# Turning the queries of a delta rule on VectorE and through DRAM instead of on TensorE, and a new order of the mixer's columns

## The chip, the cores and the metric

The kernel runs on one core of a Trainium2 chip. The core has a matrix engine (TensorE, PE in the profile, with its weight loads shown as PEld), VectorE (DVE), ScalarE (ACT), GpSimd (POOL) and SyncE (SP), which only issues transfers. Each engine works through its own list of instructions in order, and they wait for one another by semaphores. The metric is the device time of one execution in microseconds; lower is better.

## The reference

One decoder layer on 512 tokens of 1024 channels, in float32: a feed-forward block, a mixer, a second feed-forward block, a final norm. The mixer projects its input into columns and feeds two branches: a gated linear recurrence with 8 heads (HGRN2), and a gated delta rule with 8 heads of queries and keys and 16 of values. What matters here is how the queries and keys of the delta rule are normalized:

```
qkv = silu(causal_short_conv(concat([gq, gk, gv]), conv_w))
cq, ck, cv = split(qkv)
q_g = l2norm(cq.reshape(B, S, 8, 128)) * 128 ** -0.5      # x * rsqrt(sum(x*x) + eps)
k_g = l2norm(ck.reshape(B, S, 8, 128))
...
o_g = gated_delta_chunked(q_g, k_g, cv, beta, g)          # 64-token chunks in the reference
o_g = rmsnorm(o_g, gdn_out_norm) * silu(gz)
```

So for each token and each of the 8 heads a sum of 128 squares is wanted, of the key and of the query.

## The kernel before

Activations are kept with channels on the 128 partitions and the 512 tokens along the free axis. A float32 product is made of three products of split operands (high and low parts; `mm3`, lines 189 to 192). A weight block is loaded by SP into one of three `raw` tiles, split by ScalarE (line 1819) and VectorE (line 1821), and then used by TensorE.

The mixer computes its input projection column by column: a column is 128 output channels, 24 products of 128x512 into one PSUM bank of the two in lane "mm". The letters of the string `DENSE` name them: Q, F, B are the first branch's, D the decays', k, q, v the delta rule's keys, queries and values, z its output gates, y the first branch's projection; sixteen columns t (merge gates) have no place in the string. The order in `DENSE` is one of preference: `choose` takes the first column in it whose conditions hold (buffers free, a recurrence far enough), and a gate t when none does.

Everything in the mixer is written as threads (generators) that ask for buffers, wait for events and say which engine they need and about how long. At build time a planner (`Desk`) plays these threads through with its own costs, and the order in which it grants an engine becomes the order of instructions on that engine. The columns (`product`) are the thread of least urgency on TensorE and fill what the others leave. Nothing is rearranged on the chip. `V(n)`, `A(n)` and `T_(n)` are the planner's costs for VectorE, ScalarE and TensorE, `S` is one issue on SP, `LAG` holds assumed latencies, `("get", tag, n)` takes buffers of a kind, `D.put` returns them, `D.fire` tells of an event and `("on", ...)` waits for one.

A column of the delta rule goes through `conv` (line 1118): it takes two tiles of the pool `ta`, which has six, copies the product out of PSUM (line 1125), makes the short convolution and the gate. Keys and queries are written to `kq[:, c, i]`, four token blocks c, with the key (i = 0) and the query (i = 1) side by side; values are turned to tokens on partitions with `turn` and `bounce`. `turn` (line 1154) is VectorE's transpose of 32x32 blocks, and `bounce` (line 1158) writes the result to DRAM and reads it back in an order that finishes the transpose (lines 1162 and 1167, both on SP).

The eight pairs u of value heads (one query and key head each) go through these threads:

- `norms(u, i)` (line 1190) makes the sums of squares of the key (i = 0) or query (i = 1): four transposes on TensorE into the PSUM bank of lane "e" (line 1196; there is one such bank), for the key a copy of it to SBUF (line 1199), and four squares on ScalarE, each with its sum over the free axis (line 1203), in place in PSUM. Then the bank is free.
- `g_n` (line 1207) starts both, makes the coefficients from the key's sums, and multiplies keys with keys and queries (`pgq`, line 1242, also in lane "e").
- `g_b` inverts 32x32 triangular blocks on GpSimd (lines 1293 and 1294), `g_inv` joins them to 128x128 inverses on VectorE and TensorE (lines 1312 to 1370).
- `g_rec` (from line 1374) runs the recurrence over the four token blocks, and at its end scales the outputs by factors that hold the query's sums (lines 1472 to 1486).

After the last column, `closing` multiplies the delta rule's outputs with its branch projection; it needs the outputs of all pairs (`so[k]`, lines 1512, 1514, 1604, 1606).

Of the kernel before, what the change touches and what calls it, by code (L numbers as in the profile page):

```python
# [11 lines left out]
AF = mybir.ActivationFunctionType  # L12
# [6 lines left out]
NT = T // P  # L19
D = 1024  # L20
# [11 lines left out]
LEVELS = (1, 2, 4, 8, 16)  # L32

DENSE = (
# [3 lines left out]
)  # L38
MERGE = (None, None, "a", "a", "b", "b", None, None)
WB = 6  # L40
# [11 lines left out]
FRESH = 5  # L52
LAG = dict(raw=3.5, gb=6.5, nb=6, m=7, out=6.5, back=6, turn=6.5)
EASE = 2.5
LANES = {"a": 2, "b": 2, "d": 1, "e": 1}


# [84 lines left out]
def body(tc, xT, cst, sqc, hmask, dta, w1o, w1a, w2a, wt, wn, wab, wbh, wbg, wo, w1b, w2b, yT, dbg=None):  # L142
# [51 lines left out]
    def dense(src, nk, xs, m=P, n=T, lane=None):  # L194
# [3 lines left out]
        else:  # L198
            pt = psc.tile([P, T], F32, tag="p" + lane, name="pmm", bufs=LANES[lane])
        k = 0  # L200
# [154 lines left out]
    def fast(w, p, xo, fp, at, posts, gate):  # L355
# [17 lines left out]
        def prod(o, c, new=None):  # L373
            def run(hi, lo):
                if new:
                    v["pt"] = psc.tile([P, T], F32, tag="p" + new, name="px", bufs=LANES[new]) if new != "m" else \
                        psd.tile([P, T], F32, tag="mm", name="px")
# [71 lines left out]
    def ffn(w1, w2, c0, after, slow, lead=None, last=None):  # L449

        with tc.tile_pool(name="ff", bufs=1) as fp, \
# [6 lines left out]
            mm = lambda: psd.tile([P, T], F32, tag="mm", name="pmm")  # L458
            lane = lambda x: lambda: psc.tile([P, T], F32, tag="p" + x, name="pmm", bufs=LANES[x])

# [107 lines left out]
    def opening(pl):  # L568
# [17 lines left out]

        pw = psc.tile([P, T], F32, tag="pe", name="pwarm", bufs=LANES["e"])
        for i in range(11):
            pe.matmul(pw[:, :P], ones, ones, start=True, stop=True)
        pts = [psd.tile([P, T], F32, tag="mm", name="pmm") for _ in range(2)]  # L590
        pts += [psc.tile([P, T], F32, tag="pa", name="pmm", bufs=LANES["a"]) for _ in range(2)]
        parts = []
# [29 lines left out]
    def last(go, pl, units, on, hooks):  # L622
# [7 lines left out]
        for q in range(2):  # L630
# [21 lines left out]
            def scale(c=c, r=r):  # L652
                pb = psc.tile([P, T], F32, tag="pe", name="pbc", bufs=LANES["e"])
                for i in range(2):
                    pe.matmul(pb[:, i * P:(i + 1) * P], r[:, i:i + 1].to_broadcast([P, P]), ident,
                              start=True, stop=True)
                act.copy(rbc[:, c], pb[:, :256])
                for kt in range(KD):
                    g = cs[:, C_FN + kt:C_FN + kt + 1]
                    if kt % 2 == 0:  # L660
                        o = pl.tile([P, T], F32, name="rw", bufs=RW).rearrange("p (a t) -> p a t", a=2)
                    if kt in scaled:
                        pool.tensor_tensor(o[:, 1], h[:, kt, c], rbc[:, c], op=ALU.mult)
                    else:
                        dve.scalar_tensor_tensor(o[:, kt % 2], h[:, kt, c], g, pb[:, :256], op0=ALU.mult, op1=ALU.mult)
                    if kt % 2 == 1:
                        sp.dma_start(yT[:, kt - 1:kt + 1, c], o)
# [21 lines left out]
def mixer(tc, mp, e):  # L689
    nc = tc.nc  # L690
    pe, act, dve, pool, sp = nc.tensor, nc.scalar, nc.vector, nc.gpsimd, nc.sync
# [6 lines left out]
    def ps(name, lane="d"):  # L698
        return psc.tile([P, T], F32, tag="p" + lane, name=name, bufs=LANES[lane])

    def v3(ap, a):
        return ap.rearrange("p (a b) -> p a b", a=a)
# [9 lines left out]
    def alloc(tag, bufs):  # L712
        def f(name, shape=(P, T), dt=F32):
            return mp.tile(list(shape), dt, tag=tag, name=name, bufs=bufs)
        return f
    op = [alloc(f"op{i}", 1) for i in range(8)]
    ta = alloc("ta", TA)
# [3 lines left out]
    for size, names in ((1024, "n2:2 gz:2 fs:1 ut:1"), (512, "kn:3 gm:1 qm:2 gb:2 ln:1 at:4 vb:4 t64:2 on:2"),  # L721
                        (256, "ft:1 tp:1 thg:2 x:1 we:1 s:3 w:1"), (128, "fm:1"), (64, "sm:4")):
        for it in names.split():
            n, b = it.split(":")
# [35 lines left out]
    D = Desk(wx0=1, wx1=1, wx2=1, wx3=1, mm=2, a=2, b=2, d=1, e=1, ta=TA, tm=6, thg=1, raw=RB, w=WB, n2=2, gz=2, fs=1, ut=1, t=3, kn=3, gm=1,  # L760
             qm=2, gb=2, ln=1, mi=3, mt=3, at=4, vb=4, t64=2, on=2, ft=1, x=1, we=1, w_=1, s=3)
    V = lambda n: ("use", "DVE", 0.21 + 0.001 * n)
    A = lambda n: ("use", "ACT", 0.2 + 0.0009 * n)
# [169 lines left out]
    def h_head(i):  # L933
# [151 lines left out]
        dve.tensor_scalar(rho, ss, 4.0 / P, 4.0 * EPS * 4.0 * P, op0=ALU.mult, op1=ALU.add)  # L1085
        yield "lag", EASE
        yield "use", "POOL", 1.2
        pool.tensor_tensor(rho, rho, mhalf[:, :NT], op=ALU.pow)
        yield "lag", EASE
        for c in range(NT):  # L1090
# [29 lines left out]
    def conv(k, i, pt, out, n):  # L1120
# [22 lines left out]
        if n:  # L1143
            dve.scalar_tensor_tensor(out, a, 1.0, b, op0=ALU.add, op1=ALU.mult)
            D.put("ta", 2)
        else:
            dve.scalar_tensor_tensor(y, a, 1.0, b, op0=ALU.add, op1=ALU.mult)
            yield V(512)
            turn(th, y)
            D.put("ta")  # L1150
            yield from bounce(f"vn{i}", th, out, "ta")
        D.fire(k)

    def turn(out, x):

        dve.transpose(out.rearrange("p (f c j) -> p f c j", f=4, c=NT), x.rearrange("p (c i f) -> p f c i", c=NT, f=4))

    def bounce(name, x, out, tag=None):

        yield S  # L1160
        scr = dr.tile([P, T], F32, name=name)
        sp.dma_start(scr, x)
        yield "lag", LAG["turn"]
        if tag:
            D.put(tag)
        yield S
        sp.dma_start(out.rearrange("p (r a) -> p r a", r=4), scr.rearrange("(r i) (f a) -> (i f) r a", r=4, f=4))
        yield "lag", LAG["turn"]
# [20 lines left out]

    def norms(u, i, kq, kn, sm):  # L1190
        yield "on", ("kq"[i], u)
        yield "get", "e", 1
        yield T_(Patient(.5))
        pt = ps("ptk", "e")
        for c in range(NT):
            pe.transpose(pt[:, c * P:(c + 1) * P], kq[:, c, i], ident)
        if i == 0:
            yield A(512)
            act.copy(kn, v3(pt, NT))
        for c in range(NT):  # L1200
            yield A(300)
            pc = pt[:, c * P:(c + 1) * P]
            act.activation(pc, pc, AF.Square, accum_out=sm[:, 0, 4 * i + c:4 * i + c + 1])
        D.put("e")
        D.fire(("norm", u, i))

    def g_n(u, st):
# [5 lines left out]
        for i in range(2):  # L1213
            D.start((4, u, i), norms(u, i, kq, kn, sm))
# [5 lines left out]
        dve.tensor_scalar(rk, sm[:, 0, 0:4], 4.0 * EPS, None, op0=ALU.add)  # L1220
        yield "lag", EASE
        yield "use", "POOL", 1.2, 1
        pool.tensor_tensor(rk, rk, mhalf[:, :4], op=ALU.pow)
        yield "lag", EASE
        s8 = lambda i: v3(sm[:, i], NT)
# [78 lines left out]
    def g_inv(u, st):  # L1304

        yield "on", ("P", u), *([("I", u - 1)] if u else []), *([("K", u - 3)] if u > 2 else []), \
            ("ut", u % 3), ("t64", u % 2), *(["more"] if u else [])
        yield "lag", EASE
        n2 = st["n2"].rearrange("p a c b -> p (a c) b")
# [70 lines left out]
    def g_rec(u, st):  # L1380
# [34 lines left out]
        for c in range(NT):  # L1415
# [36 lines left out]
            if c < NT - 1:  # L1452
# [5 lines left out]
                else:  # L1458
                    for i in range(2):
# [14 lines left out]
                                 op0=ALU.mult, op1=ALU.add)  # L1474
        yield "lag", EASE
        yield "use", "POOL", 1.4
# [3 lines left out]
        for i in range(2):  # L1480
            yield "get", "on", 1
            ons.append(places["on"]("on", (P, NT, P)))
            to = at if u < 7 else ons
            for c in range(NT):
                yield A(150)
                act.activation(to[i][:, c], at[i][:, c], AF.Copy, scale=rho[:, 4 * i + c:4 * i + c + 1])
            if u < 7:
                yield V(512)
                turn(ons[i].rearrange("p c b -> p (c b)"), at[i].rearrange("p c b -> p (c b)"))
# [561 lines left out]
```

## Time and profile before

| | |
|---|---|
| median of 3 runs | 1600.07 us (1598.64 to 1600.56) |
| the profiled execution, its own time | 1599.18 us |
| span of that execution, first to last instruction | 1597.3 us |
| granted TensorE clock | 0.998 |
| memory traffic over the span | 220.63 MB, mean 138 GB/s |
| transposes for the sums (tile ptk) | 64 on TensorE, from 555.5 to 962.9 us |
| VectorE's block transposes in `turn` (line 1156) | 30, from 633.5 to 1081.1 us |

A row of a group reads: line, engine, operation, output tile <- input tiles, count, then minimum, median and longest duration in ns and the first and last start in us. A row of a timeline reads: start, length (both us), engine, line, operation, and in brackets the idle time of the engine before it and what ended that. A row of waits reads: who, on whom, us in total, how many times, the longest. A row of stretches reads: from and to, length, then for each engine the busy us and the number of instructions, the granted clock, the share of the DMA engines and GB/s. Lengths of matmuls overlap, since they are pipelined: what a matmul costs is read from the starts.

### The profile page before, as it was taken

The numbers are of one execution on the slowest core, as the hardware profiler recorded it, in microseconds if no ns is written. First come the engines' busy times: TensorE is split into PE (matmuls) and PEld (weight loads), VectorE is DVE, ScalarE is ACT, GpSimd is POOL, SyncE is SP. The second block draws the span as 40 slices with busy tenths as digits, with TensorE's granted clock in tenths as the row PEclk, the third lists the DMA queues.
The fourth block names the chain that finished last, engine by engine and source line by source line (L and its number), as shares of the span: only waits on it lengthen the run. The fifth ranks groups of instructions, "written<-read, shape, count | busy, mean of one in ns | idle before, by whom it ended". The sixth has DMA issues, their size and how long they took to land.

```text
span 1597.3 us, 29111 instructions
## 1 busy us (share of the span) xinstructions
PE 1582.3 (99%) x10552; PEld 1374.3 (86%) x10552; DVE 1140.7 (71%) x2220; ACT 847.6 (53%) x1912; POOL 415.9 (26%) x725
## 2 busy tenths in 40 slices
PE   9999999999999999999999999999999999999997
PEld 8899998888888888888878888888788899999887
DVE  6988785448858769746788988875545788879333
ACT  5756674334434344645766666565324666667222
POOL 0211212000312222065725676700001221121001
PEclk9999999999999999999999999999999999999999
DMA  5776873333213213555345535557543687685333
GB/s 181 173 161 157 178 169 98 117 119 108 79 55 93 61 47 110 147 159 151 114 141 157 164 120 181 180 189 220 167 128 125 148 183 159 157 184 143 93 90 118
DMA packets 141984, 220.63 MB, mean 138 GB/s; under 512 B 22144, under 2 KB 43392, under 8 KB 141840
## 3 DMA queue, kind: packets, MB, share of 16 engines
q1 hardware_dynamic: 124848, 188.14, 38.8%
q0 software_dynamic: 14400, 26.22, 10.6%
q10 hardware_dynamic: 2592, 4.42, 1.0%
q8 instruction: 83, 1.36, 0.4%
q14 instruction: 61, 0.50, 0.1%
HBM read 195.88 MB, written 22.84 MB: 137 GB/s over the span
## 4 chain that ended last, share of the span: by engine, by line
PE 90%; DMA 3%; issue 3%; DVE 1%; ACT 1%; SPq 0%; POOL 0%; POOLq 0%; ACTq 0%; DVEq 0%
PE pmm L190 19%; PE pmm L191 19%; PE pmm L192 19%; PE px L192 6%; PE px L191 6%; PE px L190 6%; PE pnat L190 2%; PE pnat L192 2%; PE pnat L191 2%; DMA wlo<-w1b 1%; DMA wlo<-w1a 1%; PE pgq L1242 1%; PE pog L1450 1%; PE pw L1434 1%; PE pl L1005 1%
## 5 line engine op out<-in xcount | busy, mean ns | idle before, releaser
L190 PE MATMUL pmm<-uh,whi 128*128 128x512 f32 x879 | 360.1, 410 | 1.4 <-ACT ci L1125 1.4
L192 PE MATMUL pmm<-uh,wlo 128*128 128x512 f32 x879 | 342.9, 390 | 0.0
L191 PE MATMUL pmm<-ul,whi 128*128 128x512 f32 x879 | 342.3, 389 | 0.5 <-DVE ul L1606 0.3
L192 PE MATMUL px<-xs,wlo 128*128 128x256 f32 x1008 | 285.8, 284 | 1.2 <-DMA wlo<-w1b 0.5
L191 PE MATMUL px<-xs,whi 128*128 128x256 f32 x1008 | 285.3, 283 | 0.0
L190 PE MATMUL px<-xs,whi 128*128 128x256 f32 x1008 | 285.3, 283 | 0.0
L1819 ACT CAST whi<-raw 128x512 fp32r<-128x512 f32 x226 | 140.1, 621 | 221.0 <-PE pmm L191 185.7
L1821 DVE TENSOR_TENSOR wlo<-raw,whi 128x512 fp32r<-128x512 f32 x226 | 160.6, 712 | 116.2 <-ACT whi L1819 113.9
L192 PEld LDWEIGHTS pmm<-uh,wlo 128*128 128x128 f32 x879 | 165.1, 188 | 35.8
L192 PEld LDWEIGHTS px<-xs,wlo 128*128 128x128 f32 x1008 | 193.5, 192 | 1.9 <-DMA wlo<-w1b 0.7
L190 PEld LDWEIGHTS pmm<-uh,whi 128*128 128x128 f32 x879 | 165.6, 188 | 34.0 <-ACT ci L1125 2.0
L190 PEld LDWEIGHTS px<-xs,whi 128*128 128x128 f32 x1008 | 193.5, 192 | 0.1
L191 PEld LDWEIGHTS px<-xs,whi 128*128 128x128 f32 x1008 | 193.5, 192 | 0.1
L191 PEld LDWEIGHTS pmm<-ul,whi 128*128 128x128 f32 x879 | 165.7, 189 | 31.0 <-DVE ul L1606 0.6
L330 ACT CAST whi<-sw 128x512 fp32r<-128x512 f32 x144 | 87.6, 613 | 92.8 <-DVE sw L367 72.9
L309 DVE TENSOR_TENSOR wlo<-raw,whi 128x512 fp32r<-128x512 f32 x100 | 77.7, 788 | 76.6 <-ACT whi L330 76.2
L330 ACT CAST whi<-raw 128x512 fp32r<-128x512 f32 x104 | 61.4, 592 | 127.2 <-PE pmm L191 92.0
L228 POOL TENSOR_TENSOR acc<-acc,sqt 128x512 f32<-128x512 f32 x18 | 23.4, 1301 | 310.6 <-ACT sqt L226 310.6
L309 DVE TENSOR_TENSOR wlo<-sw,whi 128x512 fp32r<-128x512 f32 x144 | 98.1, 682 | 0.0
L330 ACT CAST whi<-rw 128x512 fp32r<-128x512 f32 (+1 forms) x130 | 79.6, 613 | 26.1 <-PE px L191 14.0
L190 PE MATMUL pmm<-xs,whi 128*128 128x512 f32 (+1 forms) x238 | 89.8, 377 | 0.0
L191 PE MATMUL pmm<-xs,whi 128*128 128x512 f32 (+1 forms) x238 | 89.8, 377 | 0.0
(480 smaller groups left out, 3211.5 us busy)
## 6 DMA issues: line engine op xcount, KB each, us to landing
raw<-wt SPq DMA_DIRECT2D x160, 256.0 KB
rw<-w1b SPq DMA_DIRECT2D x80, 256.0 KB
rw<-w1a SPq DMA_DIRECT2D x74, 256.0 KB
wlo<-w1b POOLq DMA_DIRECT2D x53, 256.0 KB, 4.9
wlo<-w1a POOLq DMA_DIRECT2D x47, 256.0 KB, 4.9
raw<-w2b SPq DMA_DIRECT2D x41, 256.0 KB
raw<-w2a SPq DMA_DIRECT2D x36, 256.0 KB
raw<-wn SPq DMA_DIRECT2D x32, 256.0 KB
```

What stands on the lines that cost most here:

```text
L190: pe.matmul(pt, ah, bh, start=first, stop=False)
L191: pe.matmul(pt, ah, bl, start=False, stop=False)
L192: pe.matmul(pt, al, bh, start=False, stop=last)
L228: add.tensor_tensor(acc, acc, s, op=ALU.add)
L309: dve.tensor_tensor(lo, x, hi.bitcast(F32), op=ALU.subtract)
L330: act.copy(hi, x)
L1005: pe.matmul(pl_[s0:s0 + 32, c * 16:(c + 1) * 16], ke[:, c * P + s0:c * P + s0 + 32], qv[:, c, r, :, 1], start=True, stop=True)
L1242: pe.matmul(pq[:, (c % 2) * 256:(c % 2) * 256 + 256], kq[:, c, 0], kq[:, c].rearrange("p a b -> p (a b)"), start=True, stop=True)
L1434: pe.matmul(pw[:, hd2[i]], ut[:, 4 * i + c], xs[i], start=True, stop=True)
L1450: pe.matmul(po[:, 256 + i * P:256 + (i + 1) * P], at[i][:, c], w[:, hd2[i]], start=True, stop=True)
L1819: act.copy(hi, raw)
L1821: dve.tensor_tensor(lo, raw, hi.bitcast(F32), op=ALU.subtract)
```

## The change

The parameter `TURNED` names which of the two, keys (0) or queries (1), go the new way; it names the queries alone. For them `norms` takes a tile of `ta`, turns the query on VectorE into it, sends it through DRAM with `bounce` back into the same tile, and squares it there on ScalarE. The transposes of the queries on TensorE and their use of lane "e" are gone. Those of the keys stay. `turn` accepts an input of three dimensions for this. The string `DENSE` names the same columns in another order of preference.

```
 DENSE = (
-    "F0 Q0 F1 Q1 F2 Q2 F3 Q3 D0 B0 B1 F4 Q4 F5 Q5 B2 F6 Q6 F7 Q7 B3 "
-    "k0 q0 k1 q1 y0 y1 y2 y3 v0 v1 y4 y5 y6 y7 k2 q2 v2 v3 z0 z1 k3 q3 v4 v5 z2 z3 k4 q4 v6 v7 z4 z5 "
-    "k5 q5 v8 v9 z6 z7 k6 q6 v10 v11 z8 z9 k7 q7 v12 v13 z10 z11 v14 v15 z12 z13 z14 z15 "
+    "F0 Q0 F1 F2 Q1 Q2 F3 Q3 D0 B0 B1 F4 Q4 F5 Q5 B2 F6 Q6 F7 Q7 B3 k0 q0 k1 q1 y0 v0 y1 v1 y2 y3 y4 y5 "
+    "y6 y7 k2 q2 v2 v3 z0 z1 k3 q3 v4 z2 z3 k4 q4 z4 v5 v6 z5 v7 k5 q5 v8 v9 q6 z6 k6 v10 z7 z8 z9 v11 "
+    "v12 v13 k7 z10 z11 v14 q7 v15 z12 z13 z14 z15 "
 )
...
+TURNED = (1,)
...
     def turn(out, x):
 
-        dve.transpose(out.rearrange("p (f c j) -> p f c j", f=4, c=NT), x.rearrange("p (c i f) -> p f c i", c=NT, f=4))
+        dve.transpose(out.rearrange("p (f c j) -> p f c j", f=4, c=NT), v3(x, NT).rearrange("p c (i f) -> p f c i", f=4) if len(x.shape) < 3 else
+                      x.rearrange("p c (i f) -> p f c i", f=4))
...
     def norms(u, i, kq, kn, sm):
         yield "on", ("kq"[i], u)
+        if i in TURNED:
+            yield "get", "ta", 1
+            yield V(900)
+            x = ta("kt")
+            turn(x, kq[:, :, i])
+            yield from bounce(f"{'kq'[i]}n{u}", x, x)
+            x4 = x.rearrange("p (r c j) -> p c r j", r=4, c=NT)
+            if i == 0:
+                yield A(512)
+                act.copy(kn.rearrange("p c (r j) -> p c r j", r=4), x4)
+                D.fire(("kc", u))
+            for c in range(NT):
+                yield A(300)
+                act.activation(x4[:, c], x4[:, c], AF.Square, accum_out=sm[:, 0, 4 * i + c:4 * i + c + 1])
+            D.put("ta")
+            D.fire(("norm", u, i))
+            return
         yield "get", "e", 1
```

## The prediction

> **What bounds the kernel now.** I read the busy shares of the page first, then its chain, then stretches of the span.
>
> ```profile
> span 1597.3 us, 29111 instructions
> PE 1582.3 (99%) x10552; PEld 1374.3 (86%) x10552; DVE 1140.7 (71%) x2220; ACT 847.6 (53%) x1912; POOL 415.9 (26%) x725
> PE 90%; DMA 3%; issue 3%; DVE 1%; ACT 1%; SPq 0%; POOL 0%; POOLq 0%; ACTq 0%; DVEq 0%
> ```
>
> TensorE (PE) computes 99% of the span and carries 90% of the chain that ended last; no other engine is near. The profiled execution took 1599.18 us, 1.9 over its span and 0.9 under the median of the runs, 1600.07. I subtract from the median what I find in the profile.
>
> The edit lies in the mixer. Its stretches (busy us of PE, weight load, VectorE, ScalarE, GpSimd) are:
>
> ```profile
> 560.00:760.00 200.00, 199.40 (x1327) 164.80 (x1325) 138.56 (x318) 101.73 (x267) 69.26 (x153) 1.00 0.42 123
> 760.00:970.00 210.00, 208.55 (x1400) 171.98 (x1399) 180.03 (x389) 146.22 (x436) 125.95 (x274) 1.00 0.47 144
> 970.00:1130.00 160.00, 158.27 (x925) 130.59 (x924) 116.44 (x238) 91.89 (x248) 52.14 (x112) 1.00 0.60 183
> ```
>
> PE idles 0.6, 1.45 and 1.73 us there. VectorE is 69%, 86% and 73% busy, so the middle stretch is where it could become late. The waits of PE from 440 to 1140 us are all of these:
>
> ```profile
> PE pmm L190 <- ACT ci L1125: 1.4, 1, 1.4
> PE pog L1448 <- DVE x L1439: 1.2, 1, 1.2
> PE pgq L1242 <- ACT ptk L1203: 0.6, 1, 0.6
> PE pmm L191 <- DVE ul L1606: 0.3, 1, 0.3
> PE pmm L191 <- DVE ul L1514: 0.2, 1, 0.2
> ```
>
> 3.7 us in 700. So an instruction taken off PE here should shorten the span by its own time, as long as nothing else becomes late; and there is almost no waiting to win back otherwise.
>
> [...]
>
> **(a) Removed from PE: eight groups of four transposes.** For each of eight pairs of heads the kernel transposes keys and queries into a PSUM bank, on which ScalarE sums squares:
>
> ```profile
> L1196 PE MATMUL ptk<-sq,h x48: 270/272/331, 555.5 to 914.7; 128*128 128x128 f32 x48
> L1196 PE MATMUL ptk<-sq,x x16: 272/273/329, 771.1 to 962.9; 128*128 128x128 f32 x16
> L1203 ACT ACTIVATE ptk<-ptk x64: 248/262/299, 556.8 to 966.9; 128x128 f32<-128x128 f32 x64
> ```
>
> The 64 transposes are 16 groups; the change keeps the eight of the keys. Their 272 ns overlap, so I take the price from the order of starts around one group, which stands alone between products:
>
> ```profile
> 672.64 0.39 PE L191 MATMUL pmm<-oh,whi 128*128 128x512 f32 x1
> 672.87 0.39 PE L192 MATMUL pmm<-oh,wlo 128*128 128x512 f32 x1
> 673.10 0.60 PE L1196 MATMUL ptk<-sq,h 128*128 128x128 f32 x4
> 673.45 0.48 PE L190 MATMUL pmm<-oh,whi 128*128 128x512 f32 x1
> 673.77 0.40 PE L191 MATMUL pmm<-oh,whi 128*128 128x512 f32 x1
> 674.00 0.40 PE L192 MATMUL pmm<-oh,wlo 128*128 128x512 f32 x1
> ```
>
> Products start 0.23 us apart. From 672.87 to 674.00 are 1.13 us, in which three products would need 0.69: the group costs 0.44 us, 0.35 of its own and 0.09 in the step back to wide products. 8 x 0.44 = 3.5 us. The bounds are 8 x 0.35 = 2.8, if that step is paid to another small group beside it, and 8 x 0.60 = 4.8, if the whole drawn length went. I take 3.5, the start times being direct.
>
> **(b) Removed: one wait for the bank.** Lane "e" is one PSUM bank, shared by ptk and pgq, and a query's ptk holds it until its four squares are done:
>
> ```profile
> 686.83 0.18 ACT L1203 ACTIVATION_READ_ACCUMULATOR ptk<-ptk 128x1 f32 x1
> 687.07 0.70 PE L1242 MATMUL pgq<-h 128*128 128x256 f32 x2 [0.60 <-ACT ptk L1203]
> ```
>
> That is the query group of 681 us; it no longer uses the bank. Gain 0.6 us; what is next there is the keys' group before it, long done. Zero if VectorE delivers the queries later in the new order.
>
> **(c) Added on VectorE: eight transposes of 128x512.** It does the like already, for values and outputs:
>
> ```profile
> L1156 DVE STREAM_TRANSPOSE ci<-cy x16: 1078/1094/1120, 633.5 to 1039.7; 128x512 f32<-128x512 f32 x16
> L1156 DVE STREAM_TRANSPOSE on<-gat x8: 1080/1089/1105, 783.1 to 1048.1; 128x512 f32<-128x512 f32 x8
> ```
>
> 8 x 1.09 = 8.7 us. The tile ptk alone, in the middle stretch (busy us and instructions of PE, weight load, ScalarE):
>
> ```profile
> 760.00:970.00 210.00, 6.11 (x40) 4.77 (x40) 18.00 (x85) 1.00 0.47 144
> ```
>
> 40 transposes, ten groups, five of them queries': VectorE comes to 180.0 + 5.5 = 185.5 of 210 us, 88%. The source now skips the keys between the chunks of queries; no row shows that stride, and I take the same 1.09 (two times that would give 91%). On PE this costs nothing as long as it fits; behind each stand the weights' low parts, the convolutions and the small steps of the recurrence for 1.09 us. Its bound on PE is rival C.
>
> [...]
>
> **(d) ScalarE** sums as many squares as before, but out of SBUF, as it does for the outputs:
>
> ```profile
> L1410 ACT ACTIVATE sqj<-gat x32: 292/306/324, 744.6 to 1034.3; 128x128 f32<-128x128 f32 x32
> ```
>
> 306 against 262 ns, 32 times: 1.4 us more on an engine 70% busy (146.22 of 210) in the middle stretch. Nothing on the path; if ScalarE were the bound, 1.4.
>
> **(e) Added on the SP queue: sixteen transfers.** A write to DRAM and a read back for each group, as for values and outputs:
>
> ```profile
> L1162 SPq DMA_DIRECT2D vn<-ci x16: 319/338/869, 634.7 to 1041.8; - x16
> L1167 SPq DMA_DIRECT2D gvb<-vn x12: 374/385/596, 636.7 to 1048.0; - x12
> SPq L1162 <- DVE ci L1156: 12.0, 6, 5.3
> SPq L1777 <- DVE wlo L1821: 258.0, 99, 23.5
> ```
>
> Issue takes 8 x (0.34 + 0.39) = 5.8 us of SP. SP works in order: while it waits for a transposed tile (12.0 us in six cases, 5.3 the longest), the loads of weights (L1777) queue behind it, and the products wait for those. But those loads themselves stood 258 us waiting for a free buffer, 2.6 us each time: they run ahead, and a delay of some 2 us is covered; 5.3 us is nearly a column of 24 x 0.23 = 5.5. I take zero, and for the far end one such delay uncovered, 5.3 - 2.6 = 2.7 us. The DMA engines are 0.47 busy in the middle stretch, and have room for ten more transfers.
>
> **(f) The later result** hurts no one: the queries' sums go only into the scale of the pair's output, at the end of g_rec. For the last pair they are ready at 967 us today (L1203 above), and the outputs that they scale are written around 1111.87 us (row under B): more than 140 us for a bounce.
>
> **(g) The columns' order** changes no work: the list is a preference, and the loader takes the first column whose conditions hold. Late in the mixer those conditions, not the list, decide (a value's column waits for the recurrence three pairs back). It can move waits: gain at most the 1.4 + 1.2 + 0.5 = 3.1 left in the list above, loss as in C. I take zero.
>
> Sum: -3.5 - 0.6 = -4.1 us. Profiled 1599.18 - 4.1 = 1595.1; median 1600.07 - 4.1 = **1596.0**.
>
> **Rivals.** A: the new order also clears the waits that are left; -7.2, 1592.9. For it: each is a single accident of the order. Against it: another order has accidents of its own.
>
> B: the end of the mixer doesn't follow. The last pair's chain runs through GpSimd's inversions, VectorE and the recurrence; if it sets the time, PE merely waits longer in the closing products:
>
> ```profile
> 1035.95 0.76 POOL L1294 TENSOR_TENSOR gln<-gln,fm 128x8 f32<-128x8 f32 x1
> 1041.26 0.69 DVE L1312 STREAM_TRANSPOSE x<-gln 128x256 f32<-128x256 f32 x1
> 1111.87 0.40 ACT L1486 ACTIVATE on<-x,sm 128x128 f32<-128x128 f32 x1
> 1116.77 0.60 PE L1500 MATMUL pto<-sq,on 128*128 128x128 f32 x4
> 1124.13 0.50 PE L191 MATMUL pmm<-ul,whi 128*128 128x512 f32 x1 [0.22 <-DVE ul L1514]
> ```
>
> For it: the waits at 1122 and 1124 us are those of this chain's end. Against it: there are 4.5 us between inversion and its use, and 4.5 between the last scaled output and PE's transposes of it, about what is saved; PE's order, not the chain, sets them. If it holds, a half to all of the gain is gone: 1598 to 1600, middle 1599.0.
>
> C: VectorE late, and tiles "ta" short. Each query now holds one of the six ta tiles through transpose, write, read and squares; a convolution needs two before it can empty its PSUM bank. The kernel shows that stall once:
>
> ```profile
> 825.01 1.08 DVE L1156 STREAM_TRANSPOSE ci<-cy 128x512 f32<-128x512 f32 x1
> 826.13 0.59 ACT L1125 COPY ci<-pmm 128x512 f32<-128x512 f32 x1 [1.28 <-DVE ci L1156]
> 826.76 0.50 PE L190 MATMUL pmm<-uh,whi 128*128 128x512 f32 x1 [1.41 <-ACT ci L1125]
> ```
>
> A turn of values held the tile, the copy waited, and PE lost about 1.6 us (1.4 and the step after it). From three such stalls in eight queries (4.1 / 1.6 = 2.6) the gain is gone; five give +8.0 - 4.1 = +3.9, 1604.0; eight give 1608.8. With the SP delay of (e) once, five give 1606.7. For it: VectorE is 86% busy just where five of the eight fall. Against it: the 24 turns in the rows under (c) caused this stall once; eight more at that rate give a third of one.
>
> That the edit doesn't do what it says is not likely: index 1 alone is in TURNED, and 32 transposes must go.
>
> **Numbers.** A measurement of this kernel can tell about 0.2% from no change, 3.2 us. The forecast, 0.39, and A, 0.15, are faster by more: 0.54. B: 0.19, the same. C: 0.27, slower; it is given more than the rate of one in 24 would, as the whole order of engines is planned anew and every engine follows that plan in order. The range runs from a little below A (4.8 for (a), 0.6 and the 3.1 make 8.5: 1591.6) to between five and eight stalls, 1606.
>
> **What would show it.** Right: ptk x32, PE's busy time 3 to 5 us lower, no wait of pgq on ptk, L1156 with 8 more rows of about 1.09 us, PE's waits in the mixer still under 5 us. Wrong: PE waiting on ci L1125 several times (C), on ul L1514 or L1606 for microseconds (B), on weights behind SP (e), or turns of queries near 2 us.

## The result, and the profile after

The changed kernel takes 1609.49 us (median of 6 runs, 1605.71 to 1611.32), the kernel before, run beside it, 1599.65 us (6 runs, 1597.73 to 1601.04). The ratio is 1.0061 with a 95% interval from 1.0050 to 1.0072: slower by 9.8 us, where 4.1 us less were forecast. The profiled execution took 1610.75 us, 1.3 more than that median, and it is this execution that the account below explains. Its page gives the span, the busy shares and the chain that ended last:

```profile
span 1609.0 us, 29080 instructions
PE 1584.3 (98%) x10520; PEld 1372.9 (85%) x10520; DVE 1144.9 (71%) x2228; ACT 843.8 (52%) x1912; POOL 411.1 (26%) x725
PE 87%; DMA 5%; DVE 3%; issue 3%; ACT 1%; SPq 1%; POOL 0%; POOLq 0%; DVEq 0%; ACTq 0%
```

TensorE has 32 instructions fewer, as it should, and yet 2.0 us more busy time; in the chain, transfers and VectorE have taken from it. The span is 11.7 us longer. By the starts of the same steps in both traces 1.2 us of that lie before the mixer's own columns and 10.7 in the mixer, and 0.2 come back behind it (in the mixer, from its first product to the first of its output projection 796.7 us became 807.4). These are the mixer's stretches (busy us of PE, weight load, VectorE, ScalarE, GpSimd; then granted clock, DMA share, GB/s):

```profile
560.00:760.00 200.00, 198.58 (x1345) 163.86 (x1345) 139.91 (x328) 100.54 (x270) 70.48 (x155) 1.00 0.44 131
760.00:970.00 210.00, 204.50 (x1299) 168.06 (x1298) 181.16 (x388) 141.94 (x421) 118.83 (x256) 1.00 0.52 154
970.00:1140.00 170.00, 163.64 (x1003) 133.13 (x1002) 117.65 (x242) 95.28 (x266) 57.62 (x129) 0.98 0.57 176
```

PE now idles 1.4, 5.5 and 6.4 us. VectorE in the middle stretch is as busy as before (181.16 against 180.03 us), so it is no new bound. The waits of PE from 440 to 1150 us, but for two of 0.3 and 0.2 us:

```profile
PE pmm L191 <- ACT ci L1126: 5.5, 4, 2.2
PE pks L1440 <- DVE s L1480: 2.6, 1, 2.6
PE pmm L191 <- ACT tg L1567: 2.2, 1, 2.2
PE pgq L1261 <- DVE gqm L1267: 1.6, 2, 1.4
PE pmm L191 <- DVE ggz L1581: 0.9, 1, 0.9
...
```

In all 13.3 us, where it was 3.7. Nearly all of it is PE waiting for ScalarE or VectorE: for a PSUM bank to be emptied (ci, tg, ggz), or for a step of the recurrence (s). So the next question is what those two engines wait for. Some of their waits from 440 to 1150 us are for a write to DRAM that still holds a tile, which neither engine waits for in the kernel before. These are the four largest:

```profile
DVE zo L1545 <- DMA od<-zo: 6.2, 1, 6.2
ACT tg L1567 <- DMA td<-tg: 3.8, 1, 3.8
ACT tg L1567 <- DMA vn<-ci: 3.5, 1, 3.5
ACT cy L1133 <- DMA vn<-ci: 1.6, 1, 1.6
```

The 3.5 us are the costliest. The timeline of SP, ScalarE, VectorE and PE around 1020 us:

```profile
1011.24 0.51 SPq L1164 DMA_DIRECT2D vn<-ci  x1
...
1018.45 0.60 ACT L1567 ACTIVATE tg<-pmm 128x512 f32<-128x512 f32 x1 [3.46 <-DMA vn<-ci]
1019.39 0.27 ACT L1416 COPY gat<-pog 128x128 f32<-128x128 f32 x1
...
1020.37 0.35 DVE L1480 SCALAR_TENSOR_TENSOR s<-s,gx,pog 128x128 f32<-128x128 f32 x1 [0.33 <-ACT gat L1416]
...
1017.79 0.39 PE L193 MATMUL pmm<-uh,wlo 128*128 128x512 f32 x1
1020.77 1.22 PE L1440 MATMUL pks<-s,h 128*128 128x256 f32 x2 [2.59 <-DVE s L1480]
...
1024.36 0.63 PE L192 MATMUL pmm<-ul,whi 128*128 128x512 f32 x1
1024.79 0.63 PE L193 MATMUL pmm<-uh,wlo 128*128 128x512 f32 x1
...
1029.20 0.39 PE L192 MATMUL pmm<-ul,whi 128*128 128x512 f32 x1
1029.43 0.40 PE L193 MATMUL pmm<-uh,wlo 128*128 128x512 f32 x1
```

A merge gate's sigmoid (line 1567) needs a `ta` tile that a value's write to DRAM still reads. That write was issued at 1011.24 and had landed by 1018.45, after 7.2 us. ScalarE works in order, so the copies of the recurrence behind the sigmoid (line 1416) wait with it; the state `s` needs those, and PE needs the state. PE loses 2.59 us, and then, for 6.83 us up to 1027.60, its products start 0.43 us apart, not 0.23. The granted clock (third from the end) shows this second loss:

```profile
1020.00:1030.00 10.00, 9.23 (x86) 7.18 (x87) 6.23 (x14) 4.42 (x14) 8.36 (x22) 0.66 0.54 186
```

At a mean of 0.66 over 10 us, 10 x 0.34 = 3.4 us are gone. The account for the mixer is then +9.6 us of waits, +3.4 of slower clock, -3.5 for the transposes taken off, and 1.2 that I can't assign; together the 10.7.

### The profile page after: what moved, and what is told of

It is laid out like the page before. It is cut to its first block, busy times and chain, and to the rows that moved or that the text cites. A ratio compares the mean times of both kernels' runs of the same rounds, so it can differ in the third digit from the quotient of the medians.

```text
span 1609.0 us, 29080 instructions
## 1 busy us (share of the span) xinstructions
PE 1584.3 (98%) x10520; PEld 1372.9 (85%) x10520; DVE 1144.9 (71%) x2228; ACT 843.8 (52%) x1912; POOL 411.1 (26%) x725
## 4 chain that ended last, share of the span: by engine, by line
PE 87%; DMA 5%; DVE 3%; issue 3%; ACT 1%; SPq 1%; POOL 0%; POOLq 0%; DVEq 0%; ACTq 0%
PE pmm L191 18%; PE pmm L192 18%; PE pmm L193 18%; PE px L193 6%; PE px L192 6%; PE px L191 6%; DMA wlo<-w1a 2%; PE pnat L191 2%; PE pnat L193 2%; PE pnat L192 2%; PE pgq L1261 1%; PE pw L1453 1%; DMA vn<-ci 1%; PE pog L1469 1%; PE pl L1006 1%
```

## The experiments

Four theories were put to the test: T, the turned queries hold `ta` tiles and others wait for them; O, the new list `DENSE` is at fault; V (W), the added work itself on VectorE, SP or the DMA queues costs; and P, which I came to only when neither T nor O alone fitted the first runs: any edit that the planner sees makes it draw the order of all engines anew, and the order of before is one that fits the chip, with few waits, while a new one doesn't.

### Each half of the change alone

order_alone is the kernel before with the new `DENSE`, nothing else:

> The kernel before with the new list of columns, queries still transposed on TensorE. Theory T (the queries' turn makes tiles of ta scarce; ScalarE and VectorE then stand waiting for transfers to empty one, and TensorE behind them): about the time of before, 1599 to 1602 us, and no wait of ScalarE or VectorE on a transfer that writes a ta tile out. Rival O (the new order of columns is what costs): most of the +9.8 us shows here, 1605 to 1610.

turn_alone is the change with the old `DENSE`:

> The changed kernel with the old list of columns. Theory T: as slow as the changed kernel or slower, 1606 to 1614 us, with ScalarE or VectorE waiting for transfers that write ta tiles out for 8 us and more. Rival O: near before less the 3.5 us of the transposes, 1596 to 1600.

order_alone takes 1613.16 us (5 runs), ratio 1.0081 [1.0067, 1.0094] to 1599.09 before: +14.1. turn_alone takes 1608.90 us (5 runs), 1.0056 [1.0043, 1.0068]: +9.8. Either half alone loses as much as both or more, so their losses don't add. order_alone turns no query and has waits of the same kind. PE's waits in it (first rows), then two of ScalarE's:

```profile
PE pmm L190 <- ACT tg L1548: 4.4, 2, 3.4
PE pmm L190 <- ACT ci L1125: 3.0, 2, 1.8
PE pw L1434 <- DVE x L1301: 2.0, 1, 2.0
...
ACT tg L1548 <- DMA od<-zo: 7.8, 1, 7.8
ACT ci L1125 <- DMA od<-zo: 3.7, 1, 3.7
```

ScalarE again stands before a tile that a transfer still reads, this time the outputs' write od. No query is in such a tile here, so T as the only cause is out, although turn_alone has what T expected of it (ScalarE and VectorE wait 8.8 us for the write od). O as the only cause is out too, since turn_alone keeps the list and loses 9.8.

### One more tile

spare_ta is the changed kernel with a seventh `ta` tile. The planner still counts six, so that all engines' lists are the same:

```
-    ta = alloc("ta", TA)
+    ta = alloc("ta", TA + 1)
```

> The changed kernel with a seventh tile of ta on the chip, of which the planner knows nothing: every engine has the same instructions in the same order. Theory T: the waits for td<-tg, vn<-ci, od<-zo and the copies ci go, and 5 to 9 of the 9.8 us with them: 1600.5 to 1604.5. Rival V (VectorE, fuller by eight transposes, is late): no change, 1608 to 1611. Rival O: no change.

1606.72 us (5 runs), 1.0047 [1.0034, 1.0059] to before: some 2 to 3 us less than the change by the ratios and the medians, though the intervals overlap; T had expected 5 to 9. The waits of PE that are left, but for the two small ones:

```profile
PE pmm L191 <- ACT ci L1126: 5.0, 4, 2.2
PE pgq L1261 <- DVE gqm L1267: 1.1, 1, 1.1
PE pmm L191 <- DVE ggz L1581: 0.9, 1, 0.9
...
```

The two waits behind transfers, on `s` and tg, are gone: 13.3 us of waits have become 7.5. The time shows less than that, because the seventh tile has a cost of its own, some 4.4 us of products that start further apart (under before_spare_ta below). With that added back, the tile wins some 7 us, so tiles that come free too late make about half of the 9.6 + 3.4 us of waits and slower clock. That the queries hold them isn't shown to be why, since order_alone has such waits without any query in a tile. The waits on ci stay. The timeline of one of them in the changed kernel shows no tile in short supply:

```profile
831.37 0.62 ACT L1838 CAST whi<-raw 128x512 fp32r<-128x512 f32 x1 [1.12 <-PE pmm L192]
831.90 0.62 ACT L1139 ACTIVATE ci<-cy 128x512 f32<-128x512 f32 x1
832.43 0.71 ACT L1133 ACTIVATE cy<-ci,cs 128x512 f32<-128x512 f32 x1
833.16 0.59 ACT L1126 COPY ci<-pmm 128x512 f32<-128x512 f32 x1
...
833.80 0.50 PE L191 MATMUL pmm<-uh,whi 128*128 128x512 f32 x1 [2.23 <-ACT ci L1126]
```

ScalarE waits for PE to release a weight buffer (line 1838), and the copy that empties a PSUM bank stands three places behind in its list. PE runs out of banks for 2.23 us. What puts the cast ahead of the copy is the order of ScalarE's list.

### The removed work alone, the order of all else kept

no_q_transposes is the kernel before, planned as before, with the query's transposes left out and its squares summed from the query as it stands, along the wrong axis:

```
-        for c in range(NT):
+        for c in range(NT if i == 0 else 0):
...
-            act.activation(pc, pc, AF.Square, ...)
+            act.activation(pc, pc if i == 0 else kq[:, c, i], AF.Square, ...)
```

> The kernel before with the eight query groups of transposes left out of TensorE's list and nothing else moved; ScalarE squares the untransposed query, so the queries' sums are others than the reference's. This prices term (a) alone. If 0.44 us per group is right and PE is the bound: 3.5 us faster, 1595.5 to 1597. If the end of the mixer is set by the last pair's chain (rival B of the prediction): less than half of that, over 1597.9.

1596.97 us (11 runs), 0.9989 [0.9980, 0.9998]: -2.1. The starts of the same products in this trace and in before's move apart by 0.39 to 0.47 us at each removed group, 3.4 us in all; (a) had read 0.44 from one group. Only part of the 3.5 arrives, since other waits grow: PE's waits in the mixer come to 4.8 us, against 3.7.

after_no_turn is the opposite: the changed kernel, planned as changed, without the queries' turns and their transfers; the squares are again those of the unturned query.

```
-            turn(x, kq[:, :, i])
-            yield from bounce(f"{'kq'[i]}n{u}", x, x)
+            for _ in range(2):
+                yield S; yield "lag", LAG["turn"]
```

> The changed kernel under its own plan, with the queries' turn and their two transfers left out of the engines' lists; ScalarE squares the unturned query, so the queries' sums are others than the reference's. Theory P: the added work is small beside the order: at most 4 of the 9.8 us go (with the tiles of ta that come free sooner), 1605.5 to 1609.5. Rival W: most of it goes, 1597 to 1602.

1608.22 us (5 runs), 1.0060 [1.0047, 1.0072]: +8.4. PE's waits are nearly those of the change:

```profile
PE pmm L191 <- ACT ci L1126: 5.0, 4, 2.2
PE pks L1440 <- DVE s L1480: 3.0, 1, 3.0
PE pmm L191 <- ACT tg L1567: 1.7, 1, 1.7
```

So eight turns and sixteen transfers together make some 1 us of the loss, less than the intervals can tell; the rest is there without them. V falls as the main cause, and the work forecast in (c) and (e) costs little.

### A new order for its own sake

move_z7 and move_v5 are the kernel before with one column moved in the list: z7 two places later, v5 three. No work is added or removed.

```
-... z6 z7 k6 q6 v10 ...
+... z6 k6 q6 z7 v10 ...
```

> The kernel before with one column, z7, two places later in its list. No work is added or removed. Theory P: slower by 2 to 12 us, 1601 to 1611, with waits of TensorE for ScalarE's and VectorE's emptying of PSUM that before doesn't have. Rival W: as before, 1598 to 1600.5.

```
-... v4 v5 z2 z3 k4 q4 ...
+... v4 z2 z3 k4 v5 q4 ...
```

> The kernel before with one column, v5, three places later in its list. No work is added or removed. Theory P: slower by 2 to 12 us, 1601 to 1611. Rival W: as before, 1598 to 1600.5.

move_z7: 1605.12 us (5 runs), 1.0042 [1.0029, 1.0055], +5.3. move_v5: 1602.70 us (11 runs), 1.0024 [1.0015, 1.0033], +2.9. PE's first waits in move_z7:

```profile
PE pq L1344 <- ACT acc L1337: 3.1, 1, 3.1
PE pmm L188 <- DVE ci L1126: 2.7, 1, 2.7
PE pmm L188 <- ACT ci L1123: 1.4, 1, 1.4
```

The third stands in before too, the first two are new. In move_z7 PE, ScalarE and VectorE each have as many instructions as before; up to 880 us they stand in the same order, behind that in another. This is what P says: moving a column at no cost in work costs 3 to 5 us, and with order_alone and turn_alone that makes four new orders, each slower than the one of before. That every new order would lose isn't shown by four.

Waits and slower clock account for these orders as they did for the change. Take PE's waits in the mixer beyond the 3.7 us of before, and half of the time that the trace shows at clock 0.50. In order_alone these are 9.3 + 5.1 = 14.4 us, in a profiled execution whose span is 14.5 us longer than before's; in move_z7 4.9 + 1.7 = 6.6 (5.5 longer), in move_v5 2.0 + 1.7 = 3.7 (4.0 longer).

### The change in the old order

same_plan is the kernel before with its plan: the query's transposes are taken from TensorE, and a thread that costs the planner nothing adds the turn, the two transfers and the squares.

```
+    def beside(u, kq, sm):
+        free = ("use", "none", 0.0)
+        turn(x, kq[:, :, 1])
+        yield "lag", 2.5
+        yield free
+        sp.dma_start(scr, x)
+        ... (read back and four squares in the same way)
```

> The queries' sums go by VectorE and DRAM as in the change, but under the plan of the kernel before: the planner still grants what the old way asked for, the eight groups of transposes are left out of TensorE's list, and the turn, the two transfers and the four squares of each query are put in beside it without a cost, in a tile of their own. Theory P (what costs the 9.8 us is that the planner's list is drawn anew: the engines' order of before fits the chip and the new one doesn't): faster than before by 1 to 3.5 us, 1596 to 1598. Rival W (the work that was added costs it: VectorE, the transfers on SP): 1602 to 1610.

1598.82 us (11 runs), 0.9991 [0.9982, 1.0000]: -1.0. That is just above the range that P had forecast, and far below that of W: the queries' new way, with nothing else moved, is no loss. The old `DENSE` stays here, and the turned query lies in a tile of its own and not in one of ta, so this run takes away the new order and the queries' hold on ta tiles together; what a new order costs without that hold is shown by order_alone and the two moves. In its profiled execution (1601.85 us, the longest of the eleven) PE waited 2.1 us for `acc`, and the clock was 0.66 from 1008 to 1018 us. ScalarE had stood for 3.5 us before that (by its waits), until the transfer og had loaded a closing operand.

Three kernels followed that wait. before_eased is the kernel before with a seventh tile and with the second closing operand (k = 1) split 4 us later; same_plan_eased has the turned queries besides, its turned tile lying in another buffer; same_plan_late drops the seventh tile again.

```
+        if k == 1:
+            D.start((7, k, 1), later(og, a, b, gn))    # waits 4 us, then the same two instructions
```

> The kernel before, its plan kept, with two waits for transfers taken out: a seventh tile of ta on the chip, and the operand k = 1 of the closing products made 4 us later, since ScalarE stood 2.5 us for its read from DRAM in the trace of before. The queries are transposed on TensorE as before. If ScalarE's waits for transfers that land later than the plan assumes are what holds TensorE up: the waits on ci at 825 us (1.4) and on acc at 1010 us (1.2) go, 1596 to 1598. If something else is late behind them: no change, 1599 to 1601.

> The same two easings, and the queries' sums by VectorE and DRAM under the plan of before, the turned query in the tile rbc, which is idle then. Theory P: the 3.5 us of the transposes and the 2.6 us of the two waits add up, less some of each: 1593 to 1597, faster than before and than the change. Rival W (the added work is late somewhere): no faster than the kernel before with the easings alone.

> The queries' sums by VectorE and DRAM under the plan of before, the turned query in the idle tile rbc, and the operand k = 1 made 4 us later; no seventh tile of ta, so that every other tile lies where it lies in the kernel before. Theory P, with the 3.5 us of the transposes and the wait at 1010 us (1.2 in before, 2.1 in same_plan, with a slower TensorE for some us behind it) gone: 1594.5 to 1597.5, faster than both kernels. Rival W: 1598 or more.

before_eased takes 1600.84 us (11 runs), 1.0012 [1.0004, 1.0021] to 1598.77: the waits in the mixer fell from 3.7 to 0.8 us, and yet it is 2.1 us slower, a miss. same_plan_eased: 1598.52 (11 runs), 0.9998 [0.9989, 1.0007], a miss as well (1593 to 1597 was forecast). Both have the seventh tile, whose cost is shown next. same_plan_late, without the seventh tile: **1596.18 us** (9 runs), 0.9976 [0.9966, 0.9985] to 1600.21: -4.0, faster than the kernel before, and than the change by more. PE's two longest waits in its mixer:

```profile
PE pmm L190 <- ACT ci L1125: 1.4, 1, 1.4
PE pw L1456 <- DVE gx L1447: 0.8, 1, 0.8
...
```

With three small ones they come to 2.9 us. The wait of pgq on ptk (0.6) and that of pog on x (1.2) are gone. By the starts about 1.5 of its gain come at 1008 us, where that second wait was, and the rest at the removed groups; the late operand without the turned queries and without a seventh tile wasn't run, so the shares rest on one pair of traces.

before_spare_ta asks what the seventh tile alone does to the kernel before, with the same lists:

> The kernel before with nothing but a seventh tile of ta, of which the planner knows nothing; the lists of all engines are the same. In spare_ta and the two eased kernels, which have that tile, products of the operands m and so start 233 to 237 ns apart and not 227. If it is the place of the tiles behind the seventh that does this: the same spacing here, 2 to 3 us lost by it, against at most 1.4 us won at 825 us: 1599.5 to 1602, and m at 233 ns or more. If it is something else in those kernels: m at 227 ns, 1597.5 to 1599.5.

1602.54 us (11 runs), 1.0017 [1.0008, 1.0026]: +2.3, for a tile that takes 1.7 of the 3.7 us of waits away; it is a little more than was forecast for the place of the tiles. The first of the three products of the mixer's output projection, in before and in before_spare_ta:

```profile
L190 PE MATMUL pmm<-m,whi x64: 388/389/390, 1192.8 to 1235.6; 128*128 128x512 f32 x64
```

```profile
L190 PE MATMUL pmm<-m,whi x64: 392/394/398, 1195.1 to 1239.2; 128*128 128x512 f32 x64
```

From the first to the last start are 42.8 and 44.1 us. Nothing waits in that stretch; the starts of the 192 products just lie 233 ns apart (mean), not 227. The seventh tile shifts all tiles allocated behind it by 2176 bytes a partition. Other products whose operand was shifted are slower too: by the starts in both traces those of m lose 1.3 us, those of the closing operands (so) 1.4, of oh 0.9, and those into pnat 0.8, some 4.4 in all, while those of uh, which was not shifted, stay at 227 ns. Less the 1.7 us of waits, that is about the 2.3. In spare_ta the same four groups lose 4.4 us against the changed kernel, so its gain is what the tile wins less that; before_eased and same_plan_eased have the same loss; in same_plan_late, without the tile, the products of m take 42.8.

## Why the prediction was wrong, point by point

**The step that failed is (g)**, and with it the use of one forecast for work in a fixed order. It said that the columns' order changes no work and took zero, "as in C" at worst. That no work changes is true, and the zero is wrong: order_alone makes +14.1, and moving one column +2.9 or +5.3. Its other premise, that late in the mixer the conditions and not the list decide, is wrong too: moving z7 changed the order on PE, ScalarE and VectorE from about 880 us on. The same holds for the turn: adding it alone to the planned kernel makes +9.8, adding it beside the old plan -1.0. What I priced was the work; what decided was that 3.7 us of waits in 700 is a property of one order of five in-order engines, and that the planner, with its assumed latencies, found no such order again in any of the new orders tried. The prediction quoted that short list as the reason why removed work would shorten the span. It is as much the reason why a new order had little to win: 3.7 us of waits at most, and 13.3 us is what came.

**Rival C** had the place right (waits on ci, and tiles short) and the half-sentence on the order planned anew, but the wrong cause and price. VectorE became hardly fuller: 181.16 us in the middle stretch, where 185.5 was worked out; in the new order other work of VectorE fell outside that stretch. Tiles that came free late cost some 7 us by spare_ta, once that run's own loss is added back; how much of it is due to the queries in them stays open. And the costliest stall took 2.59 us of waiting and 3.4 of slower clock after it, not 1.6. Its chance, 0.27, was too low: all five orders that were planned anew, the change's among them, were slower.

**(a)** was right per group: 0.39 to 0.47 us in the trace of no_q_transposes, 3.4 for eight. What was wrong is the sum's end: in a fixed order 2.1 of the 3.5 arrived; waits that grew by 1.1 us took most of the rest. **(b)** The wait of pgq on ptk is gone, as forecast, but not the time: in the changed kernel pgq waits for gqm instead, 1.6 us.

**(c) and (d)** The new tile's main rows have the forecast durations:

```profile
L1157 DVE STREAM_TRANSPOSE kt<-h x6: 1081/1092/1122, 565.2 to 918.5; 128x512 f32<-128x512 f32 x6
L1207 ACT ACTIVATE kt<-kt x32: 292/298/313, 578.2 to 991.6; 128x128 f32<-128x128 f32 x32
```

1.09 us for a turn, the stride notwithstanding, and 0.30 for a square; that they cost PE little is what after_no_turn shows (some 1 us for the turns and the transfers, within the noise). Were both engines the bound, 1.09 us of VectorE for 0.44 us of PE, eight times, would be a loss of 5.2 us. It doesn't come: in the old order the trade is no loss in same_plan (0.9991), and with the later operand a gain in same_plan_late (0.9976).

**(e)** No product waits for weights in the list of PE's waits, so zero was right. **(f)** was right: the last squares are at 991.6 us. **A** fell: the waits grew. **B** fell: the waits on ul are 0.3 and 0.2 us, as before.

## What to carry to other kernels

Where the order of the engines is computed as a whole, an edit has two prices, its work and the new order, and here the second was the larger by far. Price the work by adding it beside a fixed plan, and the new order by an edit that changes no work; if a trace shows almost no waits, a new order has little to win and much to lose (here 3.7 us of waits, and losses of 2.9 to 14.1 us). Before counting a spare buffer as free, see whether it moves other tiles (in before_spare_ta the time went up by 2.3 us).

## What was not expected of the hardware

**A short wait cost more than itself.** After the wait of 2.59 us in the changed kernel PE's products started 0.43 us apart and not 0.23 up to 1027.35 us, and after one of 3.15 us in move_z7 up to 1016.15 us. Not every wait of 2 to 3 us shows this. The same wait on ci near 833 us, in the changed kernel and in spare_ta (granted clock third from the end):

```profile
833.00:843.00 10.00, 7.82 (x33) 6.23 (x34) 8.68 (x18) 5.98 (x17) 5.94 (x12) 1.00 0.85 272
```

```profile
833.28 0.50 PE L191 MATMUL pmm<-uh,whi 128*128 128x512 f32 x1 [2.24 <-ACT ci L1126]
...
833.00:843.00 10.00, 8.76 (x30) 6.80 (x31) 7.43 (x16) 4.94 (x13) 6.41 (x16) 0.83 0.73 245
```

2.23 us of waiting left the clock at 1.00 in the one, 2.24 us brought it to 0.83 in the other, 1.7 us in 10. The traces show a difference between the two. In the changed kernel the clock is at 0.50 from 1020.77 to 1027.60 us, 6.827 us, and half of that, 3.4135 us, goes 297.0 times into the time from the clock's first record, at 7.01 us, to the fall at 1020.77, and 467.0 times into that to its other fall, at 1601.04; in the kernel before it goes 464.0 times from the first record, at 7.00, to the one fall, at 1590.79. If the span is cut at that pace, in spare_ta so that a cut falls where its clock does, the wait of 2.23 us falls into two pieces, and the one of 2.24 us into a single one (busy us of PE, then granted clock, DMA share and GB/s; the changed kernel first, then spare_ta):

```profile
829.61:833.03 3.42, 1.95 (x9) 1.00 0.72 179
833.03:836.44 3.41, 2.64 (x12) 1.00 1.01 325
```

```profile
830.27:833.68 3.41, 1.17 (x6) 1.00 0.55 185
833.68:837.10 3.42, 3.42 (x10) 0.50 0.99 352
```

The wait of 2.59 us lies in a single piece too: of the 3.41 us before the fall at 1020.77 PE was busy for 0.82. These are three waits; how much idle time in a piece brings the clock down was not shown. The slower executions of the change are those with the lower clock: 1605.71 us at a mean of 0.997, 1611.32 at 0.994, against 1597.73 to 1601.04 us before.

**The place of tiles in SBUF** changed the spacing of TensorE's products from 227 to 233 ns (mean of the products of m, before and before_spare_ta), without any wait, for a shift of 2176 bytes. The shifted operand of these products is the one of 512 columns (m, oh, so); the weights whi and wlo lie where they lay. Why the place matters was not shown.
